# Eight transposes added to the TensorE stream of a two-block fp32 kernel: four after the last attention unit, four after the last key score

## The chip, the cores and the metric

The kernel runs on one core of one Trainium2 chip. The metric is device time in microseconds (us) of one execution; the number compared is the median of a few runs. Engines are called PE (TensorE; its weight loads are PEld), DVE (VectorE), ACT (ScalarE), POOL (GpSimd) and SP (SyncE, which here only issues DMA).

## The reference, cut to what matters

Two transformer-like blocks run one after the other on 256 tokens of width 2048, all in fp32. The first block is a large input projection, four branches (pooling, spatial gating, windowed attention with 12 units of work, convolution), a gated merge through `w_branch`, `w_out` and a layer norm. The second is a projection, a state-space and an attention group, an output projection, and a mixture of experts whose keys are scored first:

```python
q = (t @ wq).reshape(T, PEER_HEADS, 2, PEER_KEY_DIM // 2)
s1 = jnp.einsum('thd,hnd->thn', q[:, :, 0], k1).astype(jnp.float32)
s2 = jnp.einsum('thd,hnd->thn', q[:, :, 1], k2).astype(jnp.float32)
v1, i1 = lax.top_k(s1, PEER_TOPK)
...
act = jax.nn.gelu(jnp.einsum('thkd,td->thk', u[ib], tb), approximate=False)
return jnp.einsum('thk,thkd->td', gb * act, v[ib])
```

The kernel computes the expert part densely: all 16384 rows of `u` (the stage on `uT`), then all rows of `v` weighted by a sparse matrix G.

## The kernel before

**The stream.** All large weights go through PE as one long stream of chunks of 128 x 2048 fp32 (1 MB), in the order in which `add_chunks` puts them on the list `stream`. SP loads a chunk into `wr`; for each half of it ACT rounds it to `wh` (type fp32r), DVE makes the remainder `wl`. The activations are split in the same way into `XH` and `XL` (or `YH` and `YL` for `w_branch`). Each 128-row piece of a half chunk is three matmuls, always in this order: high x high (`XH,wh`), low x high (`XL,wh`), high x low (`XH,wl`), all into one PSUM tile `pm`. In most stages (`T_chunk`, `wb_chunk`) the weights are stationary and 256 token columns move. In `N_chunk` and `V_chunk` (`w_out`, part of `w_in`, the whole `v` stage) 512 columns move.

**Work beside the stream.** Everything else (attention, convolution, top-k and so on) is written as Python generators that the class `Tasks` runs in four lanes. `bg()` is called once in each half chunk, nine matmuls in (in `T_chunk` and `wb_chunk` always right after a high x low matmul), and lets the lanes go on by a step or more. What such a step puts on PE thus stands as a group of a few small matmuls or transposes between two stream matmuls. A lane's PSUM tile is `bg0` to `bg3` (from `pA(lane)`, one buffer each). A generator gives up its turn with `yield WAIT`; `yield BLOCKED` says that what it needs is not there.

**The two places.** `attn_gen(u)` makes one of 12 attention units: score matmuls (`kT,VQ`), four or so transposes of the softmax (`cst,B`; `cst` holds the identity `ident`), and, after a copy by ACT, matmuls with the values (`B,vN`). The last group `B,vN` of the last unit is the last small group on PE for over 500 us: then come the rest of the `w_in` and `w_branch` stages (256 columns) and `w_out` (512 columns). In the second block, `ev_wq(c)` runs after each of the 16 chunks of `wq`: ACT copies the result to `qp`, and one call of `bg()` later the inner `score` multiplies it with the keys (`keys,qp`, two fp32 matmuls of 128 columns, four rows in the trace) into a tile `pm`, and ACT copies columns 0 to 255 of that tile to `stg`. After the 16th score the stream goes on with 128 chunks of `uT`.

In a trace row `pm<-XH,wh` a name left of the arrow is written, the names right of it are read. PE works through its rows in the order in which they were issued.

Of the kernel before, what the change touches and what calls it, by code (L numbers as in the profile page):

```python
# [16 lines left out]
P = 128  # L17
# [32 lines left out]
GO, WAIT, BLOCKED = 0, 1, 2  # L50
# [161 lines left out]
def kern(tc, A, out):  # L212
    nc = tc.nc
    with ExitStack() as ctx:
        ctx.enter_context(tc.manual_schedule())
        _kern(tc, nc, ctx, A, out)


def _kern(tc, nc, ctx, A, out):
    tasks = Tasks(4)  # L220
    V, SC, G, PE = Meter(nc.vector, tasks, "dve"), Meter(nc.scalar, tasks, "act"), nc.gpsimd, Meter(nc.tensor, tasks, "pe")
# [18 lines left out]
    ident = cst[:, C_ID]  # L240
# [18 lines left out]
    def pA(lane):  # L259
        return pab.tile([P, 512], F32, name=f"bg{lane}")  # L260
# [460 lines left out]
        tasks.add(f"attn{u}", attn_gen(u))  # L721
    ATTN = [f"attn{u}" for u in range(12)]

    ci = 0
    for j in range(8):
        add_chunks(A["w_in"], [ci, ci + 1], [T_chunk(ev_dgate_in(j)), T_chunk(ev_dval(j))])
# [670 lines left out]
    def ev_wq(c):  # L1397
        def f(o):
            t = b3["w"].tile([P, S], F32, name="qp", bufs=3)
            SC.copy(t, o)  # L1400
            def score():
                p = pm.tile([P, 512], F32, name="pm")
                for i in range(2):
                    PE.matmul(p[:, i * P:(i + 1) * P], t[:, i * P:(i + 1) * P], b3["keys"][:, c],
                              start=True, stop=True)
                s = b3["stg"].rearrange("p a b -> p (a b)")[:, c * S:(c + 1) * S].rearrange("p (t n) -> p t n", t=2)
                SC.copy(s, p[:, :S].rearrange("p (t n) -> p t n", t=2))
                scores[c] = s
                flags["wq"] = c + 1
            later.append(lambda: later.append(score))  # L1410
        return f
# [285 lines left out]
    for hc in range(2 * len(stream)):  # L1697
        c, half = divmod(hc, 2)
# [133 lines left out]
```

## Time and profile before

| | us |
|---|---|
| median of 3 runs | 3099.87 |
| the three runs | 3096.78, 3099.87, 3105.39 |
| the profiled execution | 3101.19 |
| its span (first to last instruction) | 3099.5 |
| PE busy in the span | 3053.1 |
| DVE / ACT busy in the span | 2200.7 / 1575.3 |

The profiled execution is one run apart from the three; its own time lies 1.69 us above its span. Busy time of PE is not PE at its peak, since matmuls are pipelined and their ends are modelled: what counts for the pace of the stream is how many matmuls start in a stretch of time, not how busy PE is called there.

### The profile page before, as it was taken

What the parts mean: (1) busy time and instruction counts of PE and PEld (TensorE: products, weight loads), DVE (VectorE), ACT (ScalarE), POOL (GpSimd) and SP (SyncE); (2) the same over time, 40 slices, a digit from 0 to 9 for tenths busy, and PEclk for the clock granted to TensorE, in tenths of its full rate; (3) what the DMA queues carried; (4) which work ended last, traced back from release to release, by engine and by line L of the source; (5) the groups of instructions that cost most, each with busy time, mean ns of one, the idle gap of its engine ahead of it and who ended that gap; (6) DMA issues with size and microseconds to landing.
All of it is one profiled execution on the core that took longest, in us unless ns stands there. A gap on an engine that the chain in (4) does not pass through costs nothing.

```text
span 3099.5 us, 53098 instructions
## 1 busy us (share of the span) xinstructions
PE 3053.1 (99%) x21964; PEld 2850.0 (92%) x21964; DVE 2200.7 (71%) x3195; ACT 1575.3 (51%) x2199; POOL 223.6 (7%) x187
## 2 busy tenths in 40 slices
PE   8999999999999989999999999999999999999998
PEld 8899999999999869897899999999999888888887
DVE  8899866555555567766489989788796666666665
ACT  4443565444444445556454457667675444444444
POOL 0000000000000020100000003233130000000000
PEclk9999999999999989999999999999999999999999
DMA  7555555555555535433545655666658766666654
GB/s 274 184 198 198 179 187 187 197 190 203 182 201 191 186 127 181 173 132 131 201 150 188 221 207 202 258 244 220 257 199 327 278 239 228 250 245 248 241 216 150
DMA packets 92226, 640.61 MB, mean 207 GB/s; under 512 B 10272, under 2 KB 10448, under 8 KB 17744
## 3 DMA queue, kind: packets, MB, share of 16 engines
q1 hardware_dynamic: 78192, 559.06, 49.9%
q0 software_dynamic: 13504, 77.63, 6.9%
q8 instruction: 172, 2.82, 0.4%
q14 instruction: 70, 0.57, 0.1%
q10 hardware_dynamic: 288, 0.52, 0.0%
HBM read 601.53 MB, written 35.65 MB: 206 GB/s over the span
## 4 chain that ended last, share of the span: by engine, by line
PE 96%; DVE 1%; ACT 1%; issue 1%; POOL 0%; DMA 0%; DVEq 0%; SPq 0%; ACTq 0%
PE pm L208 92%; PE bg L208 4%; ACT wh L208 1%; DVE wl L208 0%; DVE X L208 0%; DVE XL L208 0%; POOL keys L1516 0%; DMA wr<-w_in 0%; DVE stg L208 0%; ACT XH L208 0%; DVE gb L208 0%; DVE PX L208 0%; ACT PX L208 0%; ACT keys L208 0%; POOL Ad L1567 0%
## 5 line engine op out<-in xcount | busy, mean ns | idle before, releaser
L208 DVE TENSOR_TENSOR wl<-wr,wh 128x1024 fp32r<-128x1024 f32 x1048 | 1293.9, 1237 | 824.1 <-ACT wh L208 818.9
L208 ACT CAST wh<-wr 128x1024 fp32r<-128x1024 f32 x1054 | 1108.8, 1053 | 1383.5 <-PE pm L208 1325.8
L208 PE MATMUL pm<-XH,wh 128*128 128x256 f32 x4976 | 1393.7, 280 | 8.0 <-ACT wh L208 8.0
L208 PE MATMUL pm<-XL,wh 128*128 128x256 f32 x4976 | 1383.8, 278 | 0.0
L208 PE MATMUL pm<-XH,wl 128*128 128x256 f32 x4960 | 1380.4, 278 | 0.5 <-DVE wl L208 0.5
L208 PEld LDWEIGHTS pm<-XH,wh 128*128 128x128 f32 x4976 | 941.9, 189 | 14.1 <-ACT wh L208 8.0
L208 PEld LDWEIGHTS pm<-XL,wh 128*128 128x128 f32 x4976 | 937.5, 188 | 1.0 <-issue 0.7
L208 PEld LDWEIGHTS pm<-XH,wl 128*128 128x128 f32 x4960 | 932.7, 188 | 0.9 <-DVE wl L208 0.8
L208 PE MATMUL pm<-wh,whl 128*128 128x512 f32 x1024 | 398.3, 389 | 0.0
L208 PE MATMUL pm<-wh,whh 128*128 128x512 f32 x1024 | 398.3, 389 | 0.0
L208 PE MATMUL pm<-wl,whh 128*128 128x512 f32 x1024 | 398.3, 389 | 0.0
L208 PEld LDWEIGHTS pm<-wl,whh 128*128 128x128 f32 x1024 | 192.2, 188 | 39.9
L208 PEld LDWEIGHTS pm<-wh,whh 128*128 128x128 f32 x1024 | 192.2, 188 | 39.9
L208 PEld LDWEIGHTS pm<-wh,whl 128*128 128x128 f32 x1024 | 192.2, 188 | 39.8
L208 PE MATMUL pm<-wh,XH 128*128 128x512 f32 x448 | 179.5, 401 | 3.7 <-ACT XH L208 3.7
L208 PE MATMUL pm<-wh,XL 128*128 128x512 f32 x448 | 177.1, 395 | 0.7 <-DVE XL L208 0.7
L208 PE MATMUL pm<-wl,XH 128*128 128x512 f32 x448 | 177.7, 397 | 0.0
L1516 POOL TENSOR_TENSOR keys<-cst,t 128x512 f32<-128x512 f32 x64 | 137.1, 2142 | 207.1 <-ACT ga L208 206.9
L208 PE MATMUL pm<-YH,wh 128*128 128x256 f32 x512 | 144.1, 281 | 0.0
L208 PE MATMUL pm<-YL,wh 128*128 128x256 f32 x512 | 143.7, 281 | 0.0
L208 PE MATMUL pm<-YH,wl 128*128 128x256 f32 x512 | 143.7, 281 | 0.0
L208 DVE SCALAR_TENSOR_TENSOR CV<-R,par,CV 128x256 f32<-128x256 f32 x240 | 117.0, 487 | 7.3
(288 smaller groups left out, 2368.2 us busy)
## 6 DMA issues: line engine op xcount, KB each, us to landing
wr<-w_in SPq DMA_DIRECT2D x190, 1024.0 KB, 4.8
wr<-uT SPq DMA_DIRECT2D x128, 1024.0 KB, 4.9
wr<-v SPq DMA_DIRECT2D x128, 1024.0 KB, 4.9
wr<-w_branch SPq DMA_DIRECT2D x32, 1024.0 KB, 4.8
wr<-w_out SPq DMA_DIRECT2D x32, 1024.0 KB, 4.8
wr<-wq SPq DMA_DIRECT2D x16, 1024.0 KB, 4.8
Ad<-ast POOLq DMA_DIRECT2D x16, 1024.0 KB, 5.1
Gd<-stg POOLq DMA_DIRECT2D x16, 1024.0 KB, 11.8
```

The lines of the kernel that those rows point to most:

```text
L208: return f(out, *a, **k)
L1516: G.tensor_tensor(x, it, t3[:, 0, n0:n0 + 4, None].to_broadcast([P, 4, P]), op=OP.subtract)
```

## The change

A helper `settle(p, cols)` transposes the identity by the identity into the given 128-column blocks of a PSUM tile; nobody reads the result. It is used twice, four transposes each time. A new task `settle_gen`, the last on the list of the first block, waits until all 12 attention units are done, gives up one turn more, and issues its four. In `ev_wq`, after the last of the 16 scores (`c == 15`) and its copy by ACT, four more go into columns 256 to 511 of the same tile `pm` (blocks 2, 3, 2, 3).

```diff
+    def settle(p, cols):
+        for i in cols:
+            PE.transpose(p[:, i * P:(i + 1) * P], ident, ident)
+
+    def settle_gen(ln):
+        while not all(n in tasks.done for n in ATTN):
+            yield BLOCKED
+        yield WAIT
+        settle(pA(ln), range(4))
+        yield WAIT
+    tasks.add("settle", settle_gen)
...
                 SC.copy(s, p[:, :S].rearrange("p (t n) -> p t n", t=2))
+                if c == 15:
+                    settle(p, (2, 3, 2, 3))
                 scores[c] = s
```

On PE, at the first place, in a half chunk of `w_branch` two calls of `bg()` after the last group `B,vN` (numbers tell the buffers apart), before:

```order
L208 MATMUL pm_5997<-YH_96,wh_5886 128x256
L208 MATMUL pm_5997<-YL_97,wh_5886 128x256
L208 MATMUL pm_5997<-YH_96,wl_5887 128x256
L208 MATMUL pm_5997<-YH_96,wh_5886 128x256
L208 MATMUL pm_5997<-YL_97,wh_5886 128x256
L208 MATMUL pm_5997<-YH_96,wl_5887 128x256
```

And with the change:

```order
L208 MATMUL pm_5997<-YH_96,wh_5886 128x256
L208 MATMUL pm_5997<-YL_97,wh_5886 128x256
L208 MATMUL pm_5997<-YH_96,wl_5887 128x256
L208 MATMUL bg1_6007<-cst_78 128x128 x4
L208 MATMUL pm_5997<-YH_96,wh_5886 128x256
L208 MATMUL pm_5997<-YL_97,wh_5886 128x256
```

The four transposes stand alone between two stream matmuls and wait for no other engine; 48 stream matmuls lie between the last `B,vN` and them.

On PE, at the second place, behind the 16th score (in brackets the semaphores that a row waits for), before:

```order
L208 MATMUL pm<-XL,wh 128x256
L208 MATMUL pm<-XH,wl 128x256
L208 MATMUL pm<-keys,qp 128x128 [waits Activation_49]
L208 MATMUL pm<-keys,qp 128x128
L208 MATMUL pm<-XH,wh 128x256
```

And with the change:

```order
L208 MATMUL pm<-XL,wh 128x256
L208 MATMUL pm<-XH,wl 128x256
L208 MATMUL pm<-keys,qp 128x128 [waits Activation_49]
L208 MATMUL pm<-keys,qp 128x128
L208 MATMUL pm<-cst 128x128 [waits Activation_49]
L208 MATMUL pm<-cst 128x128 x3
L208 MATMUL pm<-XH,wh 128x256
```

Here the first transpose has a wait of its own on ACT: the tile that it writes is the one that ACT's copy to `stg` reads, and the wait is for that copy. No other row of any engine moves; apart from this one wait, one later row of the first block waits for PE itself, and one stream row after the scores has lost a wait on ACT that the transposes' wait covers.

## Rows read from the trace of the kernel before

**Rows 1.** The page: busy us (share) xinstructions; the chain by engine.
```profile
PE 3053.1 (99%) x21964; PEld 2850.0 (92%) x21964; DVE 2200.7 (71%) x3195; ACT 1575.3 (51%) x2199; POOL 223.6 (7%) x187
...
PE 96%; DVE 1%; ACT 1%; issue 1%; POOL 0%; DMA 0%; DVEq 0%; SPq 0%; ACTq 0%
```
**Rows 2.** Windows view; x counts the instructions that lie in or reach into it.
```profile
core 0: us, PE busy (x) PEld busy (x) DVE busy (x) ACT busy (x) POOL busy (x), PEclk, DMA share, GB/s
99.00:530.00 431.00, 431.00 (x3517) 415.36 (x3517) 350.20 (x590) 223.45 (x326) 9.24 (x17) 1.00 0.53 189
530.00:1040.00 510.00, 510.00 (x4333) 510.00 (x4332) 274.95 (x315) 216.01 (x261) 1.59 (x3) 1.00 0.54 193
1040.00:1129.00 89.00, 89.00 (x384) 72.11 (x384) 50.46 (x56) 34.97 (x38) 1.38 (x1) 1.00 0.51 182
...
1665.00:1803.00 138.00, 138.00 (x1221) 138.00 (x1219) 128.50 (x343) 63.62 (x80) 1.60 (x3) 1.00 0.61 218
...
2394.00:3099.50 705.50, 696.98 (x3078) 576.87 (x3076) 462.06 (x515) 307.21 (x336) 19.01 (x30) 1.00 0.64 234
```
**Rows 3.** Lines of PE, 530 to 1030 us: xcount | busy us, mean ns | idle.
```profile
L208 PE MATMUL pm<-XH,wl 128*128 128x256 f32 x997 | 280.2, 281 | 0.0
```
**Rows 4.** Lines of PE, 1665 to 1802 us.
```profile
L208 PE MATMUL pm<-XL,wh 128*128 128x256 f32 x404 | 111.5, 276 | 0.0
```
**Rows 5.** Timeline of PE, last attention group: start us, us, engine, line, operation.
```profile
511.63 0.28 PE L208 MATMUL pm<-XH,wl 128*128 128x256 f32 x1
511.83 0.66 PE L208 MATMUL bg<-B,vN 128*64 128x128 f32 x8
...
512.64 0.28 PE L208 MATMUL pm<-XL,wh 128*128 128x256 f32 x1
```
**Rows 6.** Lines of PE, 506.7 to 508.1 us, then 509.9 to 511.4 us.
```profile
L208 PE MATMUL pm<-XH,wh 128*128 128x256 f32 x5 | 1.4, 276 | 0.0
...
L208 PE MATMUL pm<-XL,wh 128*128 128x256 f32 x5 | 1.4, 276 | 0.0
```
**Rows 7.** Timeline of PE, four transposes of an attention unit at 424.9 us.
```profile
424.82 0.28 PE L208 MATMUL pm<-XH,wl 128*128 128x256 f32 x1
424.94 0.60 PE L208 MATMUL bg<-cst,B 128*128 128x128 f32 x4
...
425.50 0.28 PE L208 MATMUL pm<-XL,wh 128*128 128x256 f32 x1
```
**Rows 8.** Lines of PE, 411.2 to 424.4 us, then 425.7 to 433.3 us.
```profile
L208 PE MATMUL pm<-XL,wh 128*128 128x256 f32 x39 | 11.0, 281 | 0.0
...
L208 PE MATMUL pm<-XL,wh 128*128 128x256 f32 x23 | 6.5, 281 | 0.0
```
**Rows 9.** Lines of PE, 1219.3 to 1235.3 us, then 1236.9 to 1241.2 us.
```profile
L208 PE MATMUL pm<-XL,wh 128*128 128x256 f32 x47 | 13.2, 281 | 0.0
...
L208 PE MATMUL pm<-XH,wh 128*128 128x256 f32 x14 | 3.9, 276 | 0.0
```
**Rows 10.** Lines of PE, 389.9 to 391.9 us, then 392.9 to 409 us.
```profile
L208 PE MATMUL pm<-XH,wh 128*128 128x256 f32 x7 | 1.9, 276 | 0.0
...
L208 PE MATMUL pm<-XH,wl 128*128 128x256 f32 x46 | 12.9, 281 | 0.0
```
**Rows 11.** Timeline of PE, four transposes right behind another small group.
```profile
468.65 1.09 PE L208 MATMUL bg<-B,vN 128*64 128x128 f32 x16
469.68 0.66 PE L208 MATMUL bg<-cst,B 128*128 128x128 f32 x4
470.09 0.37 PE L208 MATMUL pm<-XH,wh 128*128 128x256 f32 x1
```
**Rows 12.** Lines of PE, 470.7 to 472.6 us.
```profile
L208 PE MATMUL pm<-XH,wh 128*128 128x256 f32 x4 | 1.1, 276 | 0.0
```
**Rows 13.** Timeline of PE, the 16th score.
```profile
1663.53 0.61 PE L208 MATMUL pm<-keys,qp 128*128 128x128 f32 x4
1663.90 0.37 PE L208 MATMUL pm<-XH,wh 128*128 128x256 f32 x1
```
**Rows 14.** Timeline of ACT, its copy of the 16th score.
```profile
1664.18 0.38 ACT L208 COPY stg<-pm 128x256 f32<-128x256 f32 x1 [0.57 <-PE pm L208]
```

## The prediction, made before the kernel was run

> **What bounds the kernel now.** I read the page first: PE is busy for 99% of the span and holds 96% of the chain that ended last [rows 1]. So every nanosecond between two stream matmuls counts, and nothing that only DVE, ACT or a DMA does can count much. Then I read the windows view, not for busy time (it is full everywhere) but for how many matmuls fit into a stretch [rows 2]. From 530 to 1040 us PE takes 4333 matmuls in 510 us, 117.7 ns each. From 1665 to 1803 us it takes 1221 in 138 us, 113.0 ns each. Both are the same form (128 x 256), both at a granted clock of 1.00, both without idle time. DVE is busier in the quicker stretch (128.5 of 138 us) than in the slower (275 of 510), and the DMA share is higher too (0.61 against 0.54), so neither of them makes the slow pace. The lines view has the same split in the mean duration of one matmul: 281 ns in the slow stretch [rows 3], 276 ns in the quick one [rows 4]. I use 281 and 276 as a mark of **slow** and **quick** from here on, since it can be read in short stretches too. The pace holds for hundreds of matmuls and changes only where a small group stands between two stream matmuls. The quick stream before the last attention group (276 on both sides of the transposes before it, rows 6) is slow after that group [rows 3, 5], and stays so to 1040 us. The 512-column matmuls behind it take 89 us for 384, 231.8 ns each, while the 3078 of the last stage take 697.0 us, 226.4 ns each [rows 2].
>
> That is what the change can touch: a slow stretch of over 600 us that a small group has left behind. What the quick pace would be worth there: the transposes come 48 matmuls after the last `B,vN`, at about 512.6 + 48 x 0.1177 = 518.3 us [rows 2, 5]. From there to 1040 us are 521.7 / 0.1177 = 4432 matmuls, times 117.7 - 113.0 = 4.7 ns, 20.8 us. Behind them 384 matmuls of 512 columns times 231.8 - 226.4 = 5.4 ns, 2.1 us. In all 22.9 us, 0.74% of the time. These counts hold a few matmuls that only reach into a window, so I take 22 us.
>
> **First place, cost.** Four transposes between two stream matmuls: in rows 7 the last matmul ahead starts at 424.82, the second behind at 425.50, 0.68 us where two intervals of the stream would be 0.24. So four cost 0.44 us of PE, all of it on the path. They wait for nobody and nobody waits for them.
>
> **First place, effect.** This is what decides, and no row shows it for these very transposes. The nearest rows are the attention units' own transposes, also four of 128 x 128 fp32 that read the identity. The trace has four places where such a group stands alone between stream matmuls of 256 columns. At 424.9 us: slow before, slow after [rows 7, 8]. At 508.6 us: quick before, quick after [rows 6]. At 1235.9 us: slow before, quick after [rows 9]. At 392.1 us: quick before, slow after [rows 10]. One more stands right behind another group (so its first transpose meets no stream matmul): quick after [rows 11, 12]. So "four transposes leave the quick pace" is not what the trace says. It says three of five; and of the two that were entered at the slow pace, as here, one stayed. From PE's own timing I cannot tell from outside which of the two ours will resemble. I take the one at 424.9 us as the nearest: it was a slow stream of the same stage of the kernel, with the same kind of group ahead of it, at the same point of the three-matmul round (behind high x low), and its transposes were not held up (0.12 us from the last matmul to the first transpose). Nothing outside PE takes part at ours either, so the same entry should give the same exit. At 1235.9 us two tasks gave two transposes each, a less similar group. So my value for the gain is **0**, and both ends, 0 and 22 us, are kept for the range.
>
> A rule of the skill bears on the price. The row gives 0.44 us for four transposes [rows 7]. The Trainium skill, "TensorE: Matmul & The Clock Gate", section "Part 4: PE-mode transpose", has about 275 ns for one transpose inside a kernel. By its price, an estimate of 4 x 0.275 = 1.1 us at each place, the forecast below would be 1.3 us higher; the trace does not agree, since here they overlap, and its row is used.
>
> **Second place, cost.** Behind the 16th score the first transpose waits for ACT's copy to `stg`. Before, the stream goes on at 1663.90, while the score is still draining (it ends at 1663.53 + 0.61 = 1664.14) [rows 13]. ACT starts its copy at 1664.18 and ends at 1664.56 [rows 14]. Only then may the transposes start. The way back from ACT to PE is in no row here by itself; the way from PE to ACT took 0.04 us, and I take 0.1, with 0 and 0.3 as ends. From the first of four such transposes to the next stream matmul were 0.41 us (469.68 to 470.09, rows 11). So the stream goes on at 1664.56 + 0.1 + 0.41 = 1665.07 in place of 1663.90: **1.17 us** lost (1.07 to 1.37), and everything on PE queues behind it: the whole `uT` stream. ACT and DVE run ahead by some half chunks, so nothing else is late. Cover there is none.
>
> **Second place, effect.** The 1221 matmuls that follow run at the quick pace already [rows 2, 4], so there is nothing to gain. What can be lost: if the transposes leave the slow pace, 1221 x 4.7 = 5.7 us up to 1803 us, where the next small group comes. Since the wait has drained PE, rows 11 and 12 are the nearest (a group that met no stream matmul: quick after); I take 0, and 5.7 as the other end.
>
> **Sum**, against the profiled 3101.19 (span 3099.5): 0.44 + 1.17 - 0 = +1.6 us, 3102.8. The profiled execution lies 1.3 us above the median of the runs, 3099.87; on that median the sum is **3101.5**.
>
> **The rivals.**
> (1) *The transposes leave the quick pace at the first place.* For it: three of five groups end so, and one of the two entered slowly. Against it: the likest one does not. Time: 3101.5 - 22 = 3079.5, faster by 0.7%.
> (2) *As forecast at the first place, but the second leaves the slow pace.* For it: the transposes at 392.1 us turned a quick stream slow. Against it: rows 12. Time: 3101.5 + 5.7 = 3107.2, 0.24% above before.
> (3) *Quick at the first, slow at the second*: 3079.5 + 5.7 = 3085.2.
> (4) *Slower: the last stage is entered at another pace.* The states are handed on from group to group, and PE comes to the later stages at other moments. If the stream entered the `v` stage as it enters `w_out` now, its 3078 matmuls would take 231.8 in place of 226.4 ns: +16.6 us, 3118. It decides from 2394 us on, and it needs the last small group ahead of that stage to leave the slow pace, while before it left the quick one. Against it: many groups lie between the change and that point, with waits on other engines, and the change touches none of them.
>
> [...]
>
> **How the numbers follow.** About 0.3% (9.3 us) is what a measurement of this kernel can tell from no change. The forecast 0.46; (1) 0.34; (2) 0.08; (3) 0.05; (4) 0.07. Within 0.3%: the forecast and (2), 0.54. Faster: (1) and (3), 0.39. Slower: (4), 0.07. The likeliest is no change in the pace: 3101.5. The runs of before lie 3.1 below to 5.5 above their median. The forecast's own range with that spread is 3098 to 3107. To hold 8 in 10 the range must take in (1), 3079.5 less most of that spread: **3077 to 3107**.
>
> **What would show it.** Right: four transposes at about 518 us, 0.68 us from the stream matmul ahead to the second behind; 281 ns for a stream matmul on both sides; 4250 or so matmuls in any 500 us up to 1040. At the second place a gap of some 0.5 us on PE that ACT's copy ends, then 276. Wrong, and rival (1): 276 ns behind 519 us, some 4420 matmuls in 500 us, and 384 matmuls of `w_out` in about 87 us. Rival (2): 281 from 1665 to 1803 us. Rival (4): over 230 ns for a matmul after 2394 us. What would make all of it wrong is a pace that other things than the small groups set, so that it changes from run to run.

## The result, and the profile after

| | before | after |
|---|---|---|
| median, us | 3105.09 (five runs, among them the three of "Time and profile before"; 3096.78 to 3106.81) | 3079.07 (3076.57 to 3082.12) |
| ratio to before | | 0.9927, 95% interval 0.9914 to 0.9941 |
| span of the profiled execution, us | 3099.5 | 3080.4 |

The change makes the kernel 0.7% faster. (The ratio is worked out from all executions, not from the two medians, whose quotient is 0.9916.) The forecast was no change in the pace (3101.5); what happened is its rival (1), priced at 3079.5.

The page of after, busy us of PE and its weight loads and the count of their instructions, against [rows 1]: eight instructions more and 21.6 us less of busy time.

```profile
PE 3031.5 (98%) x21972; PEld 2829.0 (92%) x21972; DVE 2202.0 (71%) x3195; ACT 1575.4 (51%) x2199; POOL 214.6 (7%) x187
```

The windows view of after, columns as in [rows 2]: the long stretch behind the first place, `w_out`, the stretch behind the 16th key score, the last stage.

```profile
534.00:1024.50 490.50, 490.50 (x4330) 490.50 (x4329) 274.68 (x314) 216.45 (x261) 1.60 (x3) 1.00 0.57 201
1024.50:1111.50 87.00, 87.00 (x383) 71.44 (x383) 50.18 (x57) 34.38 (x36) 0.88 (x1) 1.00 0.53 187
1645.50:1785.00 139.50, 139.36 (x1230) 139.37 (x1231) 128.95 (x343) 63.59 (x80) 1.61 (x3) 1.00 0.61 217
2375.00:3080.40 705.40, 696.88 (x3077) 576.97 (x3076) 462.11 (x515) 307.20 (x336) 19.06 (x30) 1.00 0.64 234
```

In the first line PE takes 4330 matmuls in 490.5 us, 113.3 ns each; before it was 4333 in 510 us [rows 2]. Little else differs: PE has no idle time in this stretch in either, the granted clock is 1.00 in both, and DVE and ACT do the same work (274.68 and 216.45 us against 274.95 and 216.01). The last stage is what it was, 696.88 us for 3077.

The lines view shows where the pace turns: PE 516.6 to 521.6 us, ahead of the four transposes of the first place, then 530 to 1020 us, behind them (count | busy us, mean ns | idle).

```profile
L208 PE MATMUL pm<-YH,wh 128*128 128x256 f32 x10 | 2.8, 281 | 0.0
...
L208 PE MATMUL pm<-XL,wh 128*128 128x256 f32 x1008 | 278.2, 276 | 0.0
```

And the transposes themselves, in the timeline of PE:

```profile
521.90 0.29 PE L208 MATMUL pm<-YH,wl 128*128 128x256 f32 x1
522.02 0.60 PE L208 MATMUL bg<-cst 128*128 128x128 f32 x4
522.38 0.37 PE L208 MATMUL pm<-YH,wh 128*128 128x256 f32 x1
522.59 0.28 PE L208 MATMUL pm<-YL,wh 128*128 128x256 f32 x1
```

They stand between two stream matmuls and wait for nothing. Slow ahead (281 ns), quick behind (276 ns).

At the second place, the timelines of PE and of ACT (in brackets the idle time before, and what ended it):

```profile
1644.57 0.60 PE L208 MATMUL pm<-keys,qp 128*128 128x128 f32 x4
1645.64 0.66 PE L208 MATMUL pm<-cst 128*128 128x128 f32 x4 [0.46 <-ACT stg L208]
1646.05 0.37 PE L208 MATMUL pm<-XH,wh 128*128 128x256 f32 x1
```

```profile
1645.21 0.37 ACT L208 COPY stg<-pm 128x256 f32<-128x256 f32 x1 [0.53 <-PE pm L208]
```

The score starts at 1644.57 and, going by [rows 13], the stream would go on 0.37 us later, at 1644.94. It goes on at 1646.05: ACT copies until 1645.58, the transposes start 0.06 us after that and take 0.41 us to the next stream matmul. 1.11 us are lost.

**Where the 19.1 us between the two spans went**, worked out from the starts of PE's instructions in the two traces (minus: after takes less):

| stretch | us |
|---|---|
| up to the last group `B,vN` (511.83 before, 515.67 after) | +3.84 |
| from there to the first matmul of `w_out` (528.22 before, 508.98 after) | -19.24 |
| `w_out`, first to last matmul (89.37, 87.66) | -1.71 |
| up to the 16th key score | -1.86 |
| 16th score to the first transposes of the selection (139.19, 140.30) | +1.11 |
| selection up to the first group `gb,ga` | -1.22 |
| all the rest | 0.0 |

The first line is no effect of the change, which comes later in the program, and most of it is not the work of small groups either. The windows view of PE in the first stage, of before and of after (us, PE busy and count, PEclk, DMA share, GB/s), and the timeline of after ahead of it:

```profile
20.00:98.00 78.00, 78.00 (x690) 1.00 0.64 236
```

```profile
20.00:98.00 78.00, 78.00 (x665) 1.00 0.63 232
```

```profile
16.40 0.28 PE L208 MATMUL pm<-XL,wh 128*128 128x256 f32 x1
17.27 0.38 PE L208 MATMUL pm<-XH,wl 128*128 128x256 f32 x1 [0.60 <-DVE wl L208]
```

No small group stands ahead of this stage. In after the stream is quick from 12.9 to 16.4 us (113.5 ns from start to start), waits 0.60 us for DVE, and is slow behind that wait, up to 101.8 us (117.8 ns): +3.0 us. The next stretch of 256 columns, up to 195 us, is slow too: +1.8. Of the later groups, those at 392.1 and 424.9 us, which left the slow pace in [rows 8, 10], left the quick one in after: -1.0. Of the 14 traces of this document four have a slow first stage (after, `w4_first`, `m2_first`, `v_more`).

The lines -1.86 and -1.22 are not credited to the change either: over the same 14 traces the first of these stretches takes 531.8 to 534.7 us (534.11 in before), and the second takes 45.35 us in `e1_first_only` too, which has no second place.

### The profile page after: what moved, and what is told of

It is laid out like the page before. It is cut to its first block, busy times and chain, and to the rows that moved or that the text cites. A ratio compares the mean times of both kernels' runs of the same rounds, so it can differ in the third digit from the quotient of the medians.

```text
span 3080.4 us, 53114 instructions
## 1 busy us (share of the span) xinstructions
PE 3031.5 (98%) x21972; PEld 2829.0 (92%) x21972; DVE 2202.0 (71%) x3195; ACT 1575.4 (51%) x2199; POOL 214.6 (7%) x187
## 4 chain that ended last, share of the span: by engine, by line
PE 96%; DVE 1%; ACT 1%; issue 1%; DMA 0%; POOL 0%; SPq 0%; DVEq 0%; ACTq 0%
PE pm L208 92%; PE bg L208 4%; ACT wh L208 1%; DVE wl L208 0%; DMA wr<-w_in 0%; DVE X L208 0%; DVE XL L208 0%; POOL keys L1531 0%; DVE stg L208 0%; DVE gb L208 0%; ACT XH L208 0%; DVE PX L208 0%; ACT PX L208 0%; ACT keys L208 0%; SPq L433 0%
## 5 line engine op out<-in xcount | busy, mean ns | idle before, releaser
L208 ACT CAST wh<-wr 128x1024 fp32r<-128x1024 f32 x1054 | 1109.2, 1053 | 1364.4 <-PE pm L208 1307.5
L1531 POOL TENSOR_TENSOR keys<-cst,t 128x512 f32<-128x512 f32 x64 | 126.9, 1983 | 211.2 <-ACT ga L208 211.0
```

The costliest lines, as they stand in the source:

```text
L208: return f(out, *a, **k)
L1531: G.tensor_tensor(x, it, t3[:, 0, n0:n0 + 4, None].to_broadcast([P, 4, P]), op=OP.subtract)
```

## The experiments

The fences below name the place in each kernel. All edits are relative to after; "the second place" is the one behind the 16th score. All kernels but `e2_second_only` and `v_more` leave the second place out. The long stretch is read by its count: some 4121 matmuls in 530 to 1015 us is the slow pace (before itself has 4121 there), 4282 the quick one. A pace "by starts" is the time from the start of one stream matmul to the start of the next.

### One place at a time

`e1_first_only`: the second place is left out.

```diff
-                if c == 15:
-                    settle(p, (2, 3, 2, 3))
```

> Only the four transposes behind the last attention unit. Theory A (they put the slow stream on the quick pace, and PE keeps it): 276 ns for a stream matmul from the transposes to w_out, some 4425 matmuls in 500 us, time 3076 to 3088 us, 18 to 25 us under the kernel before; the stream behind the 16th score is quick or slow as it comes (0 or 5.5 us). Theory B (the gain hangs on both groups, or on other waits that moved): well above 3088 us. Theory C (the pace is set anew in each execution, by nothing in the program): times of either kind, 20 us apart, among the rounds.

Measured: 3081.97 against 3105.04 us, ratio 0.9934 (0.9911 to 0.9956). `e2_second_only`: the task is left out.

```diff
-    tasks.add("settle", settle_gen)
```

> Only the four transposes behind the 16th score. Theory A: the long stretch stays slow (281 ns from 530 to 1030 us); the second group costs 1.1 us, and gives 5.5 us back in those executions in which the stream behind the 16th score would have been slow; 3097 to 3103 us. Theory B: some 10 us or more under the kernel before.

Measured: 3099.15 us, ratio 0.9984 (0.9971 to 0.9997). The windows view of PE, first of e1, then of e2, and e2's lines from 530 to 1015 us:

```profile
530.00:1015.00 485.00, 485.00 (x4282) 1.00 0.57 201
```

```profile
530.00:1015.00 485.00, 485.00 (x4120) 1.00 0.55 193
```

```profile
L208 PE MATMUL pm<-XL,wh 128*128 128x256 f32 x957 | 268.9, 281 | 0.0
```

So the gain is the first place's: without it the stretch stays slow, and e1's interval holds the ratio of after. The second place is worth little: what it gives hangs on the pace at which the stream comes to it (see "before once more").

### How many transposes

`n2_first`, `n3_first` and `n1_first` give two, three and one at the first place. The edit of `n2_first` (the others have three blocks, and one):

```diff
-        settle(pA(ln), range(4))
+        settle(pA(ln), (0, 1))
```

> As the first-place kernel, with two transposes in place of four. If any small group that meets no wait ends the slow pace (A1): 3076 to 3088 us, as with four. If the number in the group decides how the stream goes on (A2): it may stay slow, 3097 to 3107 us; the small groups of two in the trace of the kernel before left the slow pace three times in four.

> As the first-place kernel, with three transposes in place of four. A1 (any small group will do): 3076 to 3088 us. A2 (the number decides): 3097 to 3107 us; the groups of three in the trace of the kernel before both left the slow pace.

> As the first-place kernel, with one transpose in place of four. A1 (any small group without a wait, entered from the slow pace, ends quick; two, three and four did): 3074 to 3086 us. A2 (it takes two or more, one is too short to matter): 3097 to 3110 us.

Measured ratios: two 0.9925 (0.9898 to 0.9952), three 0.9935 (0.9913 to 0.9958), one 0.9943 (0.992 to 0.9967). The number does not decide at this place. The timeline of PE in `n1_first`, and its window:

```profile
516.98 0.29 PE L208 MATMUL pm<-YH,wl 128*128 128x256 f32 x1
517.10 0.27 PE L208 MATMUL bg<-cst 128*128 128x128 f32 x1
517.13 0.37 PE L208 MATMUL pm<-YH,wh 128*128 128x256 f32 x1
517.33 0.28 PE L208 MATMUL pm<-YL,wh 128*128 128x256 f32 x1
```

```profile
530.00:1015.00 485.00, 485.00 (x4281) 1.00 0.57 201
```

With one transpose it is 0.35 us from the matmul ahead to the second behind (516.98 to 517.33), where the stream alone takes 0.24, and the pace turns.

### Waits of the attention group

The group at 424.9 us that stayed slow [rows 7, 8] reads blocks that DVE has written, so its transposes carry waits. `w4_first` gives ours such waits: DVE copies the identity, and two turns later four transposes read the copies.

```diff
-        settle(pA(ln), range(4))
+        cp = B4[ln]
+        for i in range(4):
+            V.tensor_copy(cp[:, i * P:(i + 1) * P], ident)
+        yield WAIT
+        yield WAIT
+        p = pA(ln)
+        for i in range(4):
+            PE.transpose(p[:, i * P:(i + 1) * P], cp[:, i * P:(i + 1) * P], ident)
```

> Four transposes behind the last attention unit as in the first-place kernel, but each of a block that DVE copied two turns before, so that each has a wait on DVE that is long fulfilled, as the four at 424.9 us in the trace of the kernel before, which left a slow stream slow. If fulfilled waits make no difference (A1): 3074 to 3086 us. If they are what kept that group slow (A3): 3097 to 3110 us, or executions of both kinds, some 21 us apart.

Measured: ratio 0.9946 (0.9929 to 0.9962). The group in the timeline, and the window:

```profile
527.56 0.29 PE L208 MATMUL pm<-XH,wl 128*128 128x256 f32 x1
527.69 0.60 PE L208 MATMUL bg<-cst,B 128*128 128x128 f32 x4
528.04 0.37 PE L208 MATMUL pm<-XH,wh 128*128 128x256 f32 x1
```

```profile
530.00:1015.00 485.00, 485.00 (x4282) 1.00 0.57 200
```

Quick again. Waits that are long fulfilled do not keep the stream slow here.

### Another group in the place of the transposes

`m2_first` gives two fp32 matmuls of the identity by itself (128 columns each, four rows in the trace) in place of the transposes, as a key score has two.

```diff
-        settle(pA(ln), range(4))
+        p = pA(ln)
+        for i in range(2):
+            PE.matmul(p[:, i * P:(i + 1) * P], ident, ident, start=True, stop=True)
```

> Two fp32 matmuls of 128 columns (identity by identity) in place of four transposes at the first place; no wait. If any small group does it (A1): 3074 to 3086 us; the key scores in the trace, also two fp32 matmuls, end quick whenever they are entered slow. If it takes transposes: 3097 to 3110 us.

Measured: 3101.14 us, ratio 1.0003 (0.9992 to 1.0014). A key score, also two fp32 matmuls of 128 columns, does end the slow pace (the 16th score of before stands between 117.8 ns a matmul, by starts, and a quick stream [rows 4]), and these do not. `m2_second_of_round` puts the same two behind the second matmul of a round, to see whether the place decides; its task only asks for them, and the stage on `w_branch` issues them.

```diff
                 PE.matmul(o, h[:, k], YL[:, k], start=False, stop=False)
+                if k == 3 and "two" in state:
+                    q = state.pop("two")
+                    for i in range(2):
+                        PE.matmul(q[:, i * P:(i + 1) * P], ident, ident, start=True, stop=True)
                 PE.matmul(o, l[:, k], YH[:, k], start=False, stop=k == 7)
```

> The two fp32 matmuls that left the stream slow when they stood behind the third matmul of a round, now one matmul short of a round later, behind the second (low x high). Theory K (the kind of group decides: transposes end quick, fp32 matmuls do not): slow again, 3097 to 3110 us. Theory P (kind and place in the slow stream's cycle of three decide together; here the group meets the slow stream as the key scores do, which always end it): quick, 3074 to 3090 us.

Measured: 3101.18 us, ratio 0.9998 (0.9987 to 1.0009). Its timeline, and the window, which reads the same in both kernels:

```profile
517.27 0.28 PE L208 MATMUL pm<-YL,wh 128*128 128x256 f32 x1
517.39 0.61 PE L208 MATMUL bg<-cst 128*128 128x128 f32 x4
517.75 0.36 PE L208 MATMUL pm<-YH,wl 128*128 128x256 f32 x1
```

```profile
530.00:1015.00 485.00, 485.00 (x4121) 1.00 0.54 193
```

The group costs what four transposes cost (0.68 us from the matmul ahead to the second behind, in both), in `m2_first` it stands where they stand, and the stream stays slow. So an interruption of the stream is not enough.

The slow stream can be told by its weight loads as well. Their lines, 530 to 1015 us, of before (two) and of `m2_first`:

```profile
L208 PEld LDWEIGHTS pm<-XH,wh 128*128 128x128 f32 x957 | 183.7, 192 | 0.0
L208 PEld LDWEIGHTS pm<-XH,wl 128*128 128x128 f32 x957 | 179.6, 188 | 0.0
```

```profile
L208 PEld LDWEIGHTS pm<-XH,wl 128*128 128x128 f32 x957 | 183.7, 192 | 0.0
```

One load in three is long, 192 ns against 188, and which one differs from stretch to stretch. In `m2_first` it is that of the first matmul of a round ahead of the group and that of the third behind it: the group moved the long load and did not end the pace. Ahead of the group of `m2_second_of_round` one matmul stands between the long load's and the group, as in 106 of the 111 key scores that were entered slow in the traces; in the other five, two stand between, as in `m2_first`, behind the third matmul of a round as there. All 111 turned quick. So place does not tell these two matmuls from a score.

`r1_first` asks whether it takes a change of type: one more matmul of the stream's own type (fp32r), 128 columns.

```diff
-        settle(pA(ln), range(4))
+        PE.matmul(pA(ln)[:, :P], YH[:, 0, :P], YH[:, 0, :P], start=True, stop=True)
```

> One fp32r matmul of 128 columns, the stream's own type, in place of the transposes at the first place. If a change of type is needed to end the slow pace: slow, 3097 to 3110 us. If any extra instruction shifts the stream's cycle: quick, 3074 to 3090 us.

Measured: 3077.73 us, ratio 0.9923 (0.9907 to 0.9938).

```profile
516.92 0.28 PE L208 MATMUL pm<-YH,wl 128*128 128x256 f32 x1
517.04 0.22 PE L208 MATMUL bg<-YH 128*128 128x128 f32 x1
517.10 0.34 PE L208 MATMUL pm<-YH,wh 128*128 128x256 f32 x1
517.27 0.28 PE L208 MATMUL pm<-YL,wh 128*128 128x256 f32 x1
...
517.51 0.28 PE L208 MATMUL pm<-YH,wh 128*128 128x256 f32 x1
```

```profile
530.00:1015.00 485.00, 485.00 (x4282) 1.00 0.57 201
```

No transpose and no change of type is needed: at this place one odd matmul between two rounds turns the pace. Like one transpose it takes 0.35 us from the matmul ahead to the second behind, 0.11 us more than the stream alone.

### Straight behind the last values

`d_first` gives the four transposes right behind the last group `B,vN`, with no stream matmul between, and drops the task and the second place.

```diff
+            if u == 11:
+                settle(pA((ln + 1) % 4), range(4))
             dst = GC[:, j0:j0 + nh, blk * P:(blk + 1) * P]
```

> Four transposes right behind the value matmuls of the last attention unit, with no stream matmul between the two groups. If the exit follows from the last few rows before the stream goes on (as rows 11 and 12 suggest): quick, 3074 to 3086 us. If it follows from the pace of the stream ahead of the whole group (quick there) and from all that is in it, it may stay slow: 3097 to 3110 us.

Measured: ratio 0.9954 (0.9938 to 0.9971).

```profile
510.77 0.66 PE L208 MATMUL bg<-B,vN 128*64 128x128 f32 x8
511.35 0.66 PE L208 MATMUL bg<-cst 128*128 128x128 f32 x4
511.77 0.37 PE L208 MATMUL pm<-XH,wh 128*128 128x256 f32 x1
```

Quick behind it as well (4282 matmuls in the window). No slow stretch has to come first: the stream ahead of the `B,vN` group was quick.

### More of them

`v_more` gives two at the first place; two at the second, one turn later and into a tile of their own, so that they wait for no copy; and two more pairs in stages of 512 columns (`w_in`, `w_out`) and one behind the first selection unit.

```diff
-        settle(pA(ln), range(4))
+        settle(pA(ln), range(2))
...
-                    settle(p, (2, 3, 2, 3))
+                    later.append(lambda: later.append(lambda: settle(pA(3), range(2))))
...
+            if t == 0:
+                yield WAIT
+                settle(pA(ln), range(2))
+                yield WAIT
```

> Two transposes in place of four at the first place; at the second two, one turn later and into a tile of their own, so that they do not wait for ACT; and two more at three places: in the 512-column part of w_in, in w_out, and behind the first unit that picks the experts. Theory A: at the first place as with four; at the second the loss is 0.2 us, not 1.1; behind the picking unit the stream is quick (1.6 us in those executions in which it was slow). In the 512-column stages the pace goes from 229 to 226.7 ns if it has the same two kinds of pace (1.3 us in all), else it stays. Some 2 us under the changed kernel, 3074 to 3080 us.

Measured: 3077.98 us, ratio 0.9924 (0.991 to 0.9937), which cannot be told from after. By starts, the 512-column stream ran at 228.8 to 229.9 ns ahead of the added pairs and at 228.9 behind them; the last stage's 226.7 was not reached. The pair at the second place met a quick stream, left a quick one, and stalled nothing; the pair behind the selection found the stream slow and left it quick. In this profile the first stage (to 101.8 us) ran slow, as in after.

### before once more

`before_again` is the kernel before, unchanged, in a second profiled execution, made for the one group on which the forecast rested.

> The kernel before, unchanged, profiled a second time: a second look at the step of the prediction that took the group of four transposes at 424.9 us (slow stream before it, slow after it) for a rule. Theory A (transposes behind a slow stream leave it quick, and the first trace holds the rare other outcome): if that group is again entered at 281 ns, it leaves 276. Theory B (in this very kernel that group always stays slow, and the changed kernels differ in something else): entered at 281, it leaves 281 once more. Both: the last group with the values leaves 281, and 530 to 1030 us holds 118 ns for a matmul (some 4250 in 500 us). Besides, each of the 16 key scores should turn the pace over (slow to quick, quick to slow), so that the stream behind the 16th leaves at the pace at which it came to the first: quick if the first is entered quick, slow if slow.

Measured: 3105.51 us (span 3103.8). First the lines of PE from 416 to 424.2 us and from 425.2 to 432 us, on either side of that group, then the group in the timeline:

```profile
L208 PE MATMUL pm<-XH,wl 128*128 128x256 f32 x24 | 6.7, 281 | 0.0
...
L208 PE MATMUL pm<-XH,wl 128*128 128x256 f32 x21 | 5.8, 276 | 0.0
```

```profile
424.25 0.60 PE L208 MATMUL bg<-cst,B 128*128 128x128 f32 x4
424.61 0.37 PE L208 MATMUL pm<-XH,wh 128*128 128x256 f32 x1
424.81 0.28 PE L208 MATMUL pm<-XL,wh 128*128 128x256 f32 x1
```

The same instructions of the same kernel, entered slow, end **quick** here, and ended slow in [rows 7, 8]. The windows of this execution, columns as in [rows 2]:

```profile
530.00:1030.00 500.00, 500.00 (x4247) 500.00 (x4246) 265.98 (x302) 210.67 (x254) 1.59 (x3) 1.00 0.55 193
...
1665.00:1803.00 138.00, 138.00 (x1174) 138.00 (x1173) 126.41 (x334) 60.88 (x76) 1.60 (x3) 1.00 0.58 207
```

The long stretch is slow again: the last `B,vN` group, entered quick, leaves slow. But behind the 16th score there are 1174 matmuls in the 138 us that held 1221 in [rows 2]: here that stretch is slow. From the 16th score to the first transposes of the selection it takes 144.61 us (1662.70 to 1807.31) against 139.19, so 5.4 us between two executions of one kernel.

Over the 14 traces of before, after and the experiments this can be counted, from the starts of the matmuls on either side of a group that stands alone. (A group is entered at the pace of the stream ahead of it and left at the pace behind it.) **Key scores**: 222 of them stand alone between stream matmuls, and all 222 turn the pace over, 111 from slow to quick, 111 from quick to slow. Sixteen in a row give back the pace at which the stream came to the first. That is why the stretch behind the 16th is quick in some executions and slow in others: quick in seven, slow in four of the eleven traces without the second place. **An attention unit's four transposes alone**, entered slow: 13 of 14 left quick. The one that stayed slow is the group of [rows 7, 8]. **The four of the state-space part** (`cst,XS`, as in [rows 9]), entered slow: 9 of 11. **The last group `B,vN`** and others of its form, entered quick: all 27 left slow. **The added groups at the first place**: transposes or the one fp32r matmul, all eight that met a slow stream left it quick; two fp32 matmuls, both slow. By time this holds for every execution: the 39 timed ones of kernels with transposes or the fp32r matmul there took 3074.8 to 3089.1 us, the 20 with two fp32 matmuls 3096.8 to 3108.3.

Other groups of transposes do otherwise. Two of `cst,LS` in the second block, as many as `n2_first` has and as short, were entered slow in all 14 traces and left slow in all 14. The place at 1363.8 us of before, and the lines of PE from 1360.5 to 1363.6 and from 1364.4 to 1366.6 us:

```profile
1363.67 0.28 PE L208 MATMUL pm<-XH,wl 128*128 128x256 f32 x1
1363.80 0.38 PE L208 MATMUL bg<-cst,LS 128*128 128x128 f32 x2
1363.93 0.36 PE L208 MATMUL pm<-XH,wh 128*128 128x256 f32 x1
```

```profile
L208 PE MATMUL pm<-XL,wh 128*128 128x256 f32 x8 | 2.2, 281 | 0.0
...
L208 PE MATMUL pm<-XL,wh 128*128 128x256 f32 x7 | 2.0, 281 | 0.0
```

Two and two transposes of `cst,c` and `cst,XS` (at 1218.2 us of before), entered slow in all 14, left quick in three; the three of `cst,p`, entered slow 14 times, left quick once. For twos and fours of `cst,XS` alone the long load sorts all 20 that were entered slow: the six with two matmuls between the long load's and the group stayed slow, the 14 others turned quick. But the eight added groups and the attention's 14 also had two between, and all but one turned quick. So neither the number nor the kind of the instructions nor the long load's place decides alone, and the gain is shown for the added groups where they stand, not for transposes in general.

## Why the prediction was wrong

**What bounds the kernel: right.** Two paces of one form of matmul, kept for hundreds of matmuls, was what the change acted on. The pace moved, with the clock and PE's idle time in that stretch as they were. That the pace changes "only" at small groups goes too far: the wait at 17.27 us of after turned it without one.

**What the quick pace is worth: right.** 22 us was worked out; measured are 19.2 + 1.7 = 20.9, or 21.4 with the cost of 0.45 us added back. Of the two terms the 256-column one was 20.8 and came, with that cost, to 19.7, since the paces by starts are 117.8 and 113.3 ns, not 117.7 and 113.0 (the counts of a window hold matmuls that only reach into it). The 512-column one was 2.1 and came to 1.7: by starts `w_out` went from 233.3 to 228.9 ns, not from 231.8 to 226.4. In `m2_first` it ran at 229.0 though it was entered slow, so that this part is less sure.

**First place, cost: right.** 0.44 us was predicted; from 521.90 to 522.59 are 0.69 us, less two intervals of a slow stream, 0.45.

**First place, effect: the step that failed.** The value taken for the gain was 0, from the one group that looked most like ours: "the same entry should give the same exit". The same entry does not give the same exit. That very group, entered slow in each of the other 13 traces too, ended quick in all 13, a second execution of the unchanged kernel among them; what was read as a rule was its rare outcome. Likeness of one group was given more weight than counting, and two of the likenesses were misread: the small group ahead of it (409.5 us of before) is transposes and score matmuls, not `B,vN` as ahead of ours, and the stream around it is that of `w_in`, around ours that of `w_branch`. Counting in that one trace would not have settled it: three of the five groups named ended quick, but of the fours that were entered slow one of two, and with the group at 1218.2 us, which was left out, one of three. It took a second execution and the run itself.

**Second place, cost: right.** 1.17 us was predicted for the wait on ACT's copy and the transposes behind it; 1.11 were lost. The way from ACT to PE, taken as 0.1, is 0.06.

**Second place, effect: the value holds, the reason does not.** "The 1221 matmuls that follow run at the quick pace already, so there is nothing to gain" was true of one execution. The 16 scores hand on whatever pace they are given, and in four of eleven traces that is the slow one. In the trace of after, the 16th score was entered quick; without the transposes it would have left slow, as all 111 of its kind did. They left quick, and gave 5.4 - 1.1 = 4.3 us. In `e2_second_only` the score was entered slow and would have left quick by itself, and the transposes cost 1.1. Over the eleven traces that is 5.4 x 4/11 - 1.1 = +0.9 us of gain, too little to be measured; e2's interval, whose upper end is 0.9 us below before, just reaches it.

**The rivals.** (1) is what happened, and its 3079.5 was 0.4 us off. That closeness is partly luck: it was counted from a median of 3099.87, while the five runs of before have 3105.09; the ratio's interval is a gain of 18 to 27 us. The stated range of 3077 to 3107 took the result in, because it held both ends. (2) and (3) needed a second place that leaves the slow pace: it left the quick one in each trace that has it. (4) did not come: the last stage has 226.7 ns for a matmul by starts, as before. The last sentence of the prediction, that the pace might be set by other things and change from run to run, was half true: the pace with which the stream comes to a group does change from run to run, and so does that of the first stage, which no group sets; the 5.4 us of the stretch behind the 16th score are a good part of the 10 us over which the runs of before spread. What the added transposes at the two places make of it did not change in the runs.

**What stays open.** Why two fp32 matmuls of the identity, and the two transposes of `cst,LS`, leave a slow stream slow, while the added transposes, one fp32r matmul and two fp32 matmuls of a key score end it. A score's other operands, the tile that it writes (`pm`, not `bg`) and its wait on ACT were not tried. Nor is it known what the two paces are inside PE. The long weight load goes with the slow pace and may be its cause or its effect.

## What to carry to other kernels

Where a stream has two paces with the same clock and no idle time, look for the small groups at which it turns, and weigh each by the length of stream behind it: one odd matmul at 0.1 us (four transposes at 0.45) bought some 21 us here because 600 us of stream followed. Groups of the same number and kind ended otherwise elsewhere in this kernel, so each place has to be tried. Count how a kind of group ends over all its occurrences, and over more than one execution, before a single one is taken for a rule. If a pace differs between two executions of an unchanged kernel, the stretch's matmuls times the difference are part of the spread, and no edit should be credited with it.

## What had not been expected of the hardware

- The fp32r stream of 256 columns runs at 113.3 or at 117.8 ns for a matmul, at a granted clock of 1.00 in both, and keeps the one or the other for over 4000 matmuls. By starts, the stream of 512 columns has 226.7 ns in the last stage and about 229 elsewhere; in `w_out`, entered slow, it had 233.3 in before and three other traces, and 229.0 in `m2_first`.
- One fp32r matmul of 128 columns between two rounds was enough to turn a slow stream quick at the first place (`r1_first`), and one transpose too (`n1_first`). Two fp32 matmuls of the identity were not.
- A wait of 0.60 us, with no small group, turned a quick stream slow at 17.27 us of after.
- In a slow stream one weight load in three takes 192 ns, the others 188; which of the three it is differs between stretches.
- Transposes into columns 256 to 511 of a tile waited, by a semaphore of the program, for ACT's copy of columns 0 to 255: 0.46 us of idle PE. The pair of `v_more` in a tile of its own had no such wait. Whether the chip needs this wait no run shows.
